# Attention scores on row halves of the array, and a part of the softmax scaling on ScalarE, in a two-layer decoder kernel

## The chip, the cores and the metric

The kernel runs on one core of a Trainium2 chip, in one launch. The metric is the device time of one execution in microseconds (us). A profiled execution gives a span, from the first to the last instruction, and a trace of every engine: TensorE (PE, with its weight loads shown apart as PEld), VectorE (DVE), ScalarE (ACT), GpSimd (POOL) and the queue of SyncE (SP), which issues most DMAs.

## What is computed

Two layers work on 528 tokens (16 learned meta tokens ahead of 512), 1024 wide, in float32. Each layer is a mixer and a squared-ReLU MLP, both between RMS norms. The mixer has two parallel halves: attention with 8 query heads and 2 key/value heads of width 64 and a window of 128 keys, and a short gated convolution. The attention, cut to what matters here:

```python
q = partial_rope(q, cos, sin)
k = partial_rope(k, cos, sin)
s = jnp.einsum('bnqhgd,bnkhd->bnhgqk', qb, kw) * (HEAD_DIM ** -0.5)
s = jnp.where(mask[None, :, None, None], s, -jnp.inf)
m = jnp.maximum(jnp.max(s, axis=-1, keepdims=True), sk)
e = jnp.exp(s - m)
p = e / (jnp.sum(e, axis=-1, keepdims=True) + jnp.exp(sk - m))
o = jnp.einsum('bnhgqk,bnkhd->bnqhgd', p, vw)
```

Queries come in blocks of 128 (and the 16 meta tokens); each block sees its own 128 keys and the 128 ahead of them. Query heads 0 to 3 share key head 0 (g = 0), heads 4 to 7 key head 1 (g = 1). sk is a learned sink per head.

## The kernel before

Activations lie with features on partitions and tokens along the row. Every matrix product runs in a rounded format (float32r); to keep float32 accuracy an operand is split into a rounded part "hi" and a remainder "lo", and a product is the sum hi*hi + hi*lo + lo*hi (`mm3`, L192 to L194). Weights come by DMA in halves of 128 x 512 (`prep`, L134; five buffers `wraw`), are split by a copy on ACT (L107) and a subtraction on DVE (L108), and wait in a pool of prepared tiles; `refill` issues the next ones as tiles are used up. The list `blocks` gives their order: in a layer first the tile of the keys, that of the values, four query tiles, then those of the convolution.

**Queries and keys.** The evacuation of a query tile (`q_evac`, L615) or key tile (`k_evac`, L589) goes through `rope_evac` (L543): ACT copies the product out, four small DMAs on SP swap the rotated rows, DVE multiplies and adds (L559 to L561), and a last step splits the result into hi and lo. A product of scores has only 64 features to sum over. Before the change, both parts were therefore stacked on the 128 partitions: a query head's hi on one half and its lo on the other (`q_parts`, L606), and for the keys the hi of one key head on both halves (`k_hi`) and its lo on both (`k_lo`). One score tile is then two products of depth 128 (`mm2`, L198), which sum all four combinations. The stacking costs two copies and two subtractions of 64 partitions for each query tile (L610, L613) and four and four for a key tile (L598, L603).

**Attention blocks.** A block is (i, g): 128 queries, the four query heads of one key head. `scores` (L660) makes 4 x 2 products of 128x256 into two PSUM banks; DVE adds the mask and takes the maximum (L655); `softmax` (L634) makes the exponentials with their sums on ACT (L644) and then scales each of the four tiles by the reciprocal of its sum on DVE (L650). `transp` (L684) transposes the scaled tiles on PE (L690) and splits them (L279, L280). `attend` (L695) multiplies with the values, four products of 128x512, ACT copies one half of the result (L702) and DVE adds both into z (L703). There are eight blocks in each layer; layer 0 has the meta tokens' block beside them (`meta_scores`, `meta_transp`, `meta_attend`).

**Order.** The mixer has a hand-written plan: a list of matrix products (`plan`), and `put(i, ...)` which hangs an attention step behind product i. Scores run ahead of their transposes by AHEAD blocks; the first scores stand at SCORES_AT = 4, the meta steps at +2, +5 and +6 from there. The delayed part of an evacuation or a softmax is kept in `pend` and emitted behind the next product. From the order written the framework makes each engine's queue with a planner of its own (a simulated timeline), so that queues can differ from the text. In the MLP the tiles `k_hi`, `k_lo` and `vv` and three buffers `tx` are used again as operands of a fast product (`fast`, L908).

Of the kernel before, what the change touches and what calls it, by code (L numbers as in the profile page):

```python
# [8 lines left out]
F32 = mybir.dt.float32  # L9
# [4 lines left out]
P = 128  # L14
D = 1024
KT = D // P
NM = 16
# [19 lines left out]
def trunk_kernel(ctx, tc, xT, gains, sinkb, sinkm, rope, masks, maskm, ident_in, w_in, w_out, w_up, w_down, outT):  # L37
# [22 lines left out]


    k_hi = cp.tile([P, 2, LP], F32R, name="k_hi")
    k_lo = cp.tile([P, 2, LP], F32R, name="k_lo")

# [6 lines left out]
    ct, st, r2, sws = z[:, 4, :], z[:, 5, :], z[:, 7, :], (z[:, 6, :], z[:, 3, :], z[:, 2, :])  # L71
    qm = cp.tile([P, 2, 64], F32R, name="qm")
    mk = cp.tile([P, 256], F32, name="mk")
    mkm = cp.tile([64, NM], F32, name="mkm")
# [6 lines left out]
    for l in range(2):  # L81
        blocks += [("in", l, 512), ("in", l, 640)]
        blocks += [("in", l, P * j) for j in range(4)]
        for jp in range(2):
            for base in (1280, 1792, 768):
                blocks += [("in", l, base + 256 * jp + 128 * m) for m in range(2)]
        blocks += [("out", l, m) for m in range(8)]
        for c in range(NCH):
            if c:
                blocks += [("upx", l, (8 * c + 2 * m, n)) for m in range(4) for n in range(7)]  # L90
            else:
                blocks += [("up", l, 8 * c + m) for m in range(8)]
            blocks += [("down", l, (c, m)) for m in range(8)]
# [40 lines left out]
    def prep(beside=None):  # L134
# [388 lines left out]
    class Mixer:  # L523
# [19 lines left out]
        def rope_evac(self, parts, r, meta=None):  # L543
            t0, t1 = r

            def ev(ps):
# [10 lines left out]
                def rest():  # L557
                    u = tmp(n)
                    DVE.tensor_tensor(u, sw, st[:, t0:t1], ALU.mult)  # L559
                    DVE.tensor_tensor(raw, raw, ct[:, t0:t1], ALU.mult)  # L560
                    DVE.tensor_tensor(raw, raw, u, ALU.add)  # L561
                    parts(raw)
                    if meta is not None:
                        c = 2 * (meta % 2) * NM
                        self.q_parts([qm[:, meta // 2, c + n * NM:c + n * NM + NM] for n in range(2)], raw[:, 0:NM])
                pend.append(rest)
# [22 lines left out]
        def k_evac(self, n):  # L589
            t0, t1 = (RA, RB)[n]  # L590
            cols = slice(PAD + t0, PAD + t1)

            def parts(raw):
                for half in (0, 1):
                    for g in range(2):
                        src = slice(64 * g, 64 * g + 64)
                        dst = src if half == 0 else slice(64 - 64 * g, P - 64 * g)
                        ACT.activation(k_hi[dst, g, cols], raw[src], AF.Copy)  # L598
                for half in (0, 1):
                    for g in range(2):  # L600
                        src = slice(64 * g, 64 * g + 64)
                        dst = src if half == 0 else slice(64 - 64 * g, P - 64 * g)
                        DVE.tensor_tensor(k_lo[dst, g, cols], raw[src], k_hi[src, g, cols].bitcast(F32), ALU.subtract)  # L603
            return self.rope_evac(parts, (t0, t1))

        def q_parts(self, q, raw):  # L606

            for g in range(2):
                src = slice(64 * g, 64 * g + 64)
                ACT.activation(q[g][src], raw[src], AF.Copy)  # L610
            for g in range(2):
                src, dst = slice(64 * g, 64 * g + 64), slice(64 - 64 * g, P - 64 * g)
                DVE.tensor_tensor(q[g][dst], raw[src], q[g][src].bitcast(F32), ALU.subtract)  # L613

        def q_evac(self, j, n):  # L615
            t0, t1 = self.xr[n]
            q = [f[:, j, t0:t1] for f in (f_hi, f_lo)]
            return self.rope_evac(lambda raw: self.q_parts(q, raw), (t0, t1), j if t0 == 0 else None)

# [5 lines left out]
    def mixer(l, mx, mlp_first):  # L625
# [8 lines left out]
        def softmax(S, nh, sink, rows, keys, mxt):  # L634
# [24 lines left out]

        def scores(i, g):  # L660
            S = wp.tile([P, 4, L // 2], F32, tag="x", name="S", bufs=3)[:, :, :256]
# [4 lines left out]
            if i == 0:  # L666
                POOL.memset(S[:, :, :PAD], 0.0)
            for jp in range(2):
                bk = bank()
                for jj in range(2):  # L670
                    j = 2 * jp + jj
                    sc = bk[:, jj * 256:(jj + 1) * 256]
                    q = (f_hi, f_lo)[j % 2][:, 2 * g + j // 2, q0:q0 + 128]
                    mm2(sc, (q, q), (k_hi[:, g, ks], k_lo[:, g, ks]), True, True)
                for jj in range(2):
                    j = 2 * jp + jj
                    masked(S[:, j, keys], bk[:, jj * 256:(jj + 1) * 256][:, keys], mk[:, keys], mxt[:, j:j + 1])
            softmax(S, 4, sb[:, l, 4 * g:4 * g + 4], P, keys, mxt)
            sbufs[(i, g)] = S

        def pT():
            return wp.tile([P, 2, 512], F32R, tag="w", name="p", bufs=2 * CAP)

        def transp(i, g):  # L684
            S = sbufs.pop((i, g))
            pbufs[(i, g)] = []
            for kb in range(2):
# [4 lines left out]
                split(p[:, 0, :], p[:, 1, :], bk)  # L692
                pbufs[(i, g)].append((p[:, 0, :], p[:, 1, :]))

        def attend(i, g):  # L695
            ybk = bank()
            for kb, (phi, plo) in enumerate(pbufs.pop((i, g))):
                mm2(ybk, (vv[:, i + kb, g, :],) * 2, (phi, plo), kb == 0, kb == 1)
            q0 = NM + 128 * i
            rows = slice(g * 64, (g + 1) * 64)  # L700
            y = pT()[:64, 0].bitcast(F32)
            ACT.activation(y, ybk[64:P], AF.Copy)  # L702
            DVE.tensor_tensor(yat[rows, 0:4, q0:q0 + 128], ybk[:64].rearrange("p (j q) -> p j q", j=4),  # L703
                              y.rearrange("p (j q) -> p j q", j=4), ALU.add)

        def meta_scores():
            S = stile(256)[:64].rearrange("p (a b) -> p a b", a=2)
            mxt = tp.tile([P, 4], F32, tag="mx", name="mx", bufs=4)[:64, :2]
            keys = slice(PAD, P)
            POOL.memset(S[:, :, :PAD], 0.0)  # L710
            for g in range(2):
                bk = bank()
                mm2(bk[:64, 0:P], (qm[:, g, :],) * 2, (k_hi[:, g, 0:P], k_lo[:, g, 0:P]), True, True)
                masked(S[:, g, keys], bk[:64, keys], mkm, mxt[:, g:g + 1])
            softmax(S, 2, sm[:, l, :], 64, keys, mxt)
# [112 lines left out]

        order = [(i, g) for i in range(4) for g in range(2)]
        S = [lambda i=i, g=g: scores(i, g) for i, g in order]  # L830
        T = [lambda i=i, g=g: transp(i, g) for i, g in order]
        A = [lambda i=i, g=g: attend(i, g) for i, g in order]
        put(0, mx.v_later[0])
# [74 lines left out]
    def fast(l):  # L908
# [4 lines left out]
        view = lambda t: t.rearrange("p a b -> p (a b)")[:, :4 * n].rearrange("p (k t) -> p k t", k=4)  # L913
        tv = [view(k_hi), view(k_lo), view(vv.rearrange("p a b c -> p a (b c)"))] + [t[:, :, :n] for t in txs[l]]
        T = {"T1": (a_hi[:, 0:4, N1], a_lo[:, 0:4, N1]), "T2": tv[0:2], "T3": tv[2:4], "T4": tv[4:6]}
# [103 lines left out]
    def clear_pad():  # L1019
        for t in (k_hi, k_lo):  # L1020
            POOL.memset(t[:, :, :PAD].bitcast(F32), 0.0)

# [82 lines left out]
```

## Time and profile before

| | us |
|---|---|
| median of 3 runs (1110.06 to 1112.1) | 1111.5 |
| the profiled execution | 1113.09 |
| its span | 1111.3 |
| PE busy | 1079.6 |
| DVE busy | 819.8 |
| ACT busy | 627.0 |

The profile counts an engine as busy while an instruction runs. Products are pipelined: each lasts longer in the records than the distance to the next, so the pace is read from the starts. [...] A wait is the idle time of an engine ahead of an instruction, with what ended it. Idle time of an engine on which nobody waits costs nothing.

### The profile page before, as it was taken

The page shows a single profiled execution, that of the slowest core. Times are in us where ns is not written, and L with a number is a line of the kernel's source. Part 1 is how long each engine was busy: PE and PEld are TensorE (multiplying, and loading weights), DVE is VectorE, ACT ScalarE, POOL GpSimd, SP SyncE. Part 2 cuts the span into 40 slices and gives each one's busy share as a digit, 9 for nine tenths or more (in the row PEclk, how much of TensorE's full clock was granted, in tenths as well). Part 3 has the DMA queues.
Part 4 walks back from the last instruction along what each step waited for, and adds up shares of the span by engine and source line. Part 5 has one row for each costly group of instructions (what it writes and reads, how often), then busy time and mean ns, then how long its engine had stood idle before and what let it go on. Part 6 is the DMA issues. An engine that isn't in the chain of part 4 may idle for free.

```text
span 1111.3 us, 21393 instructions
## 1 busy us (share of the span) xinstructions
PE 1079.6 (97%) x8066; PEld 1038.4 (93%) x8066; DVE 819.8 (74%) x1943; ACT 627.0 (56%) x1510; POOL 11.2 (1%) x46
## 2 busy tenths in 40 slices
PE   8979999999999999999999899999999999999995
PEld 8979999999999999999988899999889989989995
DVE  7997985978486586486598989869947757757835
ACT  8665656675473274176355656666735725724732
POOL 2000000000000000000000000000000000000000
PEclk9999999999999999999998999999999999999998
DMA  9141231342243143234131322222522522522402
GB/s 260 50 126 56 58 96 58 96 134 77 58 131 99 58 122 117 58 105 138 35 112 42 108 59 77 77 76 77 152 67 77 161 67 73 152 73 75 143 1 76
DMA packets 197608, 102.04 MB, mean 92 GB/s; under 512 B 7360, under 2 KB 197456, under 8 KB 197504
## 3 DMA queue, kind: packets, MB, share of 16 engines
q1 hardware_dynamic: 196640, 99.88, 31.1%
q8 instruction: 63, 1.03, 0.4%
q10 hardware_dynamic: 688, 0.58, 0.2%
q14 instruction: 41, 0.34, 0.1%
q0 software_dynamic: 176, 0.21, 0.1%
HBM read 97.88 MB, written 2.10 MB: 90 GB/s over the span
## 4 chain that ended last, share of the span: by engine, by line
PE 83%; DVE 10%; ACT 2%; DMA 2%; issue 2%; SPq 1%; DVEq 0%; ACTq 0%
PE ps L193 26%; PE ps L194 26%; PE ps L192 26%; PE ps L198 2%; PE ps L690 1%; DVE wlo L108 1%; DVE a_lo L334 1%; DVE h L323 1%; DVE acc L276 1%; DMA h<-in_xT 1%; PE ps L231 1%; DMA wraw<-in_w_in 1%; DMA z<-t 0%; ACT whi L107 0%; DVE t L322 0%
## 5 line engine op out<-in xcount | busy, mean ns | idle before, releaser
L193 PE MATMUL ps<-f_lo,whi 128*128 128x256 f32 (+2 forms) x1072 | 326.4, 306 | 0.0
L194 PE MATMUL ps<-f_hi,wlo 128*128 128x256 f32 (+2 forms) x1072 | 326.0, 305 | 0.0
L192 PE MATMUL ps<-f_hi,whi 128*128 128x256 f32 (+2 forms) x1072 | 323.3, 306 | 0.0
L193 PE MATMUL ps<-a_lo,whi 128*128 128x256 f32 (+3 forms) x808 | 232.9, 292 | 1.8 <-DVE a_lo L334 1.7
L192 PE MATMUL ps<-a_hi,whi 128*128 128x256 f32 (+3 forms) x808 | 229.0, 297 | 5.8 <-DVE vv L280 2.6
L194 PE MATMUL ps<-a_hi,wlo 128*128 128x256 f32 (+3 forms) x808 | 231.7, 291 | 0.0
L194 PEld LDWEIGHTS ps<-f_hi,wlo 128*128 128x128 f32 x1072 | 202.0, 189 | 9.2
L108 DVE TENSOR_TENSOR wlo<-wraw,whi 128x512 fp32r<-128x512 f32 x264 | 173.4, 686 | 49.9 <-ACT whi L107 29.0
L193 PEld LDWEIGHTS ps<-f_lo,whi 128*128 128x128 f32 x1072 | 201.4, 188 | 9.4
L192 PEld LDWEIGHTS ps<-f_hi,whi 128*128 128x128 f32 x1072 | 199.9, 188 | 9.3
L107 ACT ACTIVATE whi<-wraw 128x512 fp32r<-128x512 f32 x264 | 153.6, 624 | 86.4 <-PE ps L193 54.6
L193 PEld LDWEIGHTS ps<-a_lo,whi 128*128 128x128 f32 x808 | 155.6, 193 | 5.5 <-DVE a_lo L334 2.6
L192 PEld LDWEIGHTS ps<-a_hi,whi 128*128 128x128 f32 x808 | 151.1, 193 | 9.3 <-DVE vv L280 2.8
L194 PEld LDWEIGHTS ps<-a_hi,wlo 128*128 128x128 f32 x808 | 155.6, 193 | 1.6 <-DVE wlo L108 0.2
L506 DVE TENSOR_TENSOR z<-z,ps 128x272 f32<-128x272 f32 (+2 forms) x78 | 38.0, 487 | 99.1 <-PE ps L194 98.8
L193 PE MATMUL ps<-a_lo,wf 128*128 128x264 f32 (+1 forms) x384 | 108.2, 283 | 0.0
L192 PE MATMUL ps<-a_hi,wf 128*128 128x264 f32 (+1 forms) x384 | 107.9, 283 | 0.0
L107 ACT ACTIVATE wf<-wraw 128x512 fp32r<-128x512 f32 x96 | 59.7, 626 | 84.7 <-PE ps L193 51.8
L194 PE MATMUL ps<-a_hi,wf 128*128 128x264 f32 (+1 forms) x384 | 107.1, 283 | 0.0
L107 ACT ACTIVATE wf<-u 128x512 fp32r<-128x512 f32 x72 | 45.1, 627 | 88.1 <-PE ps L193 73.6
L108 DVE TENSOR_TENSOR wf<-wraw,wf 128x512 fp32r<-128x512 f32 x96 | 65.6, 687 | 11.3 <-ACT wf L107 10.1
L193 PEld LDWEIGHTS ps<-a_lo,wf 128*128 128x128 f32 x384 | 72.2, 188 | 0.1
(175 smaller groups left out, 1815.6 us busy)
## 6 DMA issues: line engine op xcount, KB each, us to landing
wraw<-in_w_up SPq DMA_DIRECT2D x128, 256.0 KB
wraw<-in_w_down SPq DMA_DIRECT2D x128, 256.0 KB
wraw<-in_w_in SPq DMA_DIRECT2D x72, 256.0 KB
wraw<-in_w_out SPq DMA_DIRECT2D x32, 128.0 KB
wraw<-in_w_out SPq DMA_DIRECT2D x16, 256.0 KB
h<-in_xT SPq DMA_DIRECT2D x4, 272.0 KB
h<-in_xT SPq DMA_DIRECT2D x4, 256.0 KB
outT<-h SPq DMA_DIRECT2D x8, 128.0 KB
```

Of the source, the lines that this page charges most:

```text
L107: ACT.activation(hi, raw, AF.Copy)
L108: DVE.tensor_tensor(lo, raw, hi.bitcast(F32), ALU.subtract)
L192: PE.matmul(ps, whi, ahi, start=first, stop=False, skip_group_check=onto)
L193: PE.matmul(ps, whi, alo, start=False, stop=False, skip_group_check=onto)
L194: PE.matmul(ps, wlo, ahi, start=False, stop=last, skip_group_check=onto)
L198: PE.matmul(ps, a[n], b[n], start=first and n == 0, stop=last and n == 1)
L231: PE.matmul(ps, ones[:, which, :], acc, start=True, stop=more is None)
L276: return (eng or DVE).tensor_tensor(acc, acc, sq, ALU.add)
L323: DVE.tensor_tensor(hk, hk, t, ALU.add)
L334: DVE.scalar_tensor_tensor(a_lo[:, k, t0:t1], hk, g, a_hi[:, k, t0:t1].bitcast(F32), ALU.mult, ALU.subtract)
L506: DVE.tensor_tensor(zz, zz, ps, ALU.add)
L690: PE.transpose(bk[:, j * P:(j + 1) * P], S[:, j, kb * P:(kb + 1) * P], ident)
```

## The change

Query tiles now hold head j of both key heads: 64 columns of one and 64 of the other (a new kind "q" of weight block, read by two DMAs a half, each with rows of 64 columns). The hi and lo parts of queries and keys lie in tiles of their own on all 128 partitions, key head 0 on partitions 0 to 63 and key head 1 on 64 to 127, so that a split is one copy and one subtraction. A block is (i, jp): two query heads of each key head. Its scores are three products (hi*hi, hi*lo, lo*hi) of depth 64 for each head, and the products of the two key heads alternate, one on rows 0 to 63 with its bank, the other on rows 64 to 127 with another bank. Of the four scalings two go to ACT. `attend` makes eight products of 256 columns in place of four of 512, and adds to z in two instructions. The meta transposition and attend move by three slots. A constant tile `tx` takes the place of the second key tile among the operands of the fast product.

```diff
-    k_hi = cp.tile([P, 2, LP], F32R, name="k_hi")
-    k_lo = cp.tile([P, 2, LP], F32R, name="k_lo")
+    kk = cp.tile([P, 2, LP], F32R, name="kk")
+    k_hi, k_lo = kk[:, 0, :], kk[:, 1, :]
...
-        blocks += [("in", l, P * j) for j in range(4)]
+        blocks += [("q", l, j) for j in range(4)]
...
+            elif kind == "q":
+                for g in range(2):
+                    last_load[:] = [dma(raw[:, :, 64 * g:64 * g + 64], w_in[l].rearrange("(k p) m -> p k m", p=P)[
+                        :, ks, 256 * g + 64 * sub:256 * g + 64 * sub + 64])]
...
             def parts(raw):
...
+                split(k_hi[:, cols], k_lo[:, cols], raw)
...
-            return self.rope_evac(lambda raw: self.q_parts(q, raw), (t0, t1), j if t0 == 0 else None)
+            return self.rope_evac(lambda raw: split(f_hi[:, j, t0:t1], f_lo[:, j, t0:t1], raw), (t0, t1), j if t0 == 0 else None)
...
                 for i in range(nh):
-                    DVE.tensor_scalar(S[:, i, keys], S[:, i, keys], dn[:, i:i + 1], None, ALU.mult)
+                    if i % 2 and nh == 4:
+                        ACT.activation(S[:, i, keys], S[:, i, keys], AF.Copy, scale=dn[:, i:i + 1])
+                    else:
+                        DVE.tensor_scalar(S[:, i, keys], S[:, i, keys], dn[:, i:i + 1], None, ALU.mult)
...
+        def mm3_heads(outs, q, k):
+
+            for n, (a, b) in enumerate(((0, 0), (0, 1), (1, 0))):
+                for g in range(2):
+                    rows = slice(64 * g, 64 * g + 64)
+                    PE.matmul(outs[g], q[a][rows], k[b][rows], start=n == 0, stop=n == 2)
...
+            bks = [bank() for _ in range(2)]
+            for jj in range(2):
+                mm3_heads([bk[:, jj * 256:(jj + 1) * 256] for bk in bks],
+                          [f[:, 2 * jp + jj, q0:q0 + 128] for f in (f_hi, f_lo)], (k_hi[:, ks], k_lo[:, ks]))
...
+            ps = pbufs.pop((i, jp))
+            for g in range(2):
+                cols = slice(256 * g, 256 * g + 256)
+                for kb, (phi, plo) in enumerate(ps):
+                    mm2(ybk[:, cols], (vv[:, i + kb, g, :],) * 2, (phi[:, cols], plo[:, cols]), kb == 0, kb == 1)
...
-            put(at + 5, meta_transp)
-            put(at + 6, meta_attend)
+            put(at + 8, meta_transp)
+            put(at + 9, meta_attend)
```

## Rows read from the trace of the kernel before

**Rows 1.** The page, part 1: busy us, share and instructions of each engine.
```profile
PE 1079.6 (97%) x8066; PEld 1038.4 (93%) x8066; DVE 819.8 (74%) x1943; ACT 627.0 (56%) x1510; POOL 11.2 (1%) x46
```
**Rows 2.** Waits of PE: for whom, us in total, times, longest.
```profile
PE ps L722 <- DVE s L650: 4.0, 1, 4.0
PE ps L198 <- DVE f_hi L613: 3.9, 1, 3.9
PE ps L192 <- DVE vv L280: 2.6, 1, 2.6
PE ps L690 <- DVE S L650: 2.4, 1, 2.4
...
PE ps L192 <- ACT acc L297: 1.4, 1, 1.4
```
**Rows 3.** Busy time by stretch: us, PE, PEld, DVE, ACT, POOL, granted clock, DMA, GB/s.
```profile
36.00:72.00 36.00, 34.78 (x289) 34.56 (x288) 34.95 (x114) 22.66 (x60) 0.20 (x2) 1.00 0.44 123
74.60:77.90 3.30, 3.30 (x18) 3.30 (x17) 2.76 (x13) 2.89 (x13) 0.10 (x1) 0.50 0.00 0
82.70:88.40 5.70, 5.70 (x21) 4.83 (x21) 2.77 (x13) 0.00 (x0) 0.10 (x1) 0.51 0.31 92
580.00:584.00 4.00, 2.65 (x21) 2.28 (x20) 3.61 (x11) 2.17 (x6) 0.00 (x0) 1.00 0.27 70
600.90:607.00 6.10, 6.08 (x28) 6.08 (x29) 5.97 (x15) 4.90 (x12) 0.00 (x0) 0.50 0.48 136
610.00:624.00 14.00, 10.13 (x85) 9.93 (x85) 13.40 (x48) 8.54 (x26) 0.03 (x1) 1.00 0.32 88
624.20:627.60 3.40, 3.40 (x18) 3.40 (x17) 3.24 (x10) 2.98 (x6) 0.00 (x0) 0.50 0.27 74
```
**Rows 4.** Groups by line and shape on DVE: busy us, mean ns, idle before.
```profile
L280 DVE TENSOR_TENSOR f_lo<-t,f_hi 128x256 fp32r<-128x256 f32 x66 | 27.0, 420 | 3.1 <-ACT f_hi L279 3.1
...
L650 DVE TENSOR_SCALAR S<-S,dn 128x256 f32<-128x256 f32 x48 | 13.7, 349 | 0.2
...
L613 DVE TENSOR_TENSOR f_lo<-t,f_lo 64x256 fp32r<-64x256 f32 x12 | 5.1, 421 | 0.3
```
**Rows 5.** Groups by line and shape on ACT: busy us, mean ns, idle before.
```profile
L644 ACT ACTIVATE S<-S,ng 128x256 f32<-128x256 f32 x48 | 23.8, 499 | 2.9 <-DVE ng L640 2.9
...
L644 ACT ACTIVATION_READ_ACCUMULATOR S<-S,ng 128x1 f32 x64 | 12.1, 189 | 0.0
...
L702 ACT ACTIVATE p<-ps 64x512 f32<-64x512 f32 x16 | 9.6, 597 | 24.0 <-PE ps L198 23.9
...
L763 ACT ACTIVATE z<-u,gt 128x256 f32<-128x256 f32 x12 | 6.1, 506 | 12.7 <-DVE u L757 12.7
```
**Rows 6.** Timeline of DVE at the split of V in layer 1.
```profile
600.32 0.55 DVE L280 TENSOR_TENSOR vv<-ps,vv 128x384 fp32r<-128x384 f32 x1
```
**Rows 7.** Timeline of PE: start, us, instruction; scores, transposes, attend in layer 0.
```profile
55.84 0.28 PE L198 MATMUL ps<-k_hi,f_hi 128*128 128x256 f32 x1
...
56.76 0.28 PE L192 MATMUL ps<-a_hi,whi 128*128 128x256 f32 x1
...
99.68 1.03 PE L690 MATMUL ps<-ident,S 128*128 128x128 f32 x8
100.47 0.36 PE L192 MATMUL ps<-a_hi,whi 128*128 128x256 f32 x1
100.67 0.28 PE L193 MATMUL ps<-a_lo,whi 128*128 128x256 f32 x1
...
106.11 0.62 PE L198 MATMUL ps<-p,vv 128*128 128x512 f32 x2
106.57 0.29 PE L192 MATMUL ps<-a_hi,whi 128*128 128x272 f32 x1
```
**Rows 8.** The page's DMA queues, and busy time of 8 to 24 us.
```profile
q1 hardware_dynamic: 196640, 99.88, 31.1%
...
8.00:24.00 16.00, 14.90 (x102) 14.39 (x102) 14.75 (x33) 14.98 (x38) 0.00 (x0) 0.89 1.09 308
```

More of the change, by code (lines that the diff above doesn't have):

```diff
@@ L563, in rest @@
                     if meta is not None:
-                        c = 2 * (meta % 2) * NM
-                        self.q_parts([qm[:, meta // 2, c + n * NM:c + n * NM + NM] for n in range(2)], raw[:, 0:NM])
+                        cs = slice(meta * NM, meta * NM + NM)
+                        split(qm[:, 0, cs], qm[:, 1, cs], raw[:, 0:NM])
                 pend.append(rest)
@@ L667, in scores, with transp @@
                 POOL.memset(S[:, :, :PAD], 0.0)
-            for jp in range(2):
-                bk = bank()
-                for jj in range(2):
[L671 to L679, printed above, removed]
+            bks = [bank() for _ in range(2)]
[3 more added lines that the diff above has]
+            for g in range(2):
+                for jj in range(2):
+                    n = 2 * g + jj
+                    masked(S[:, n, keys], bks[g][:, jj * 256:(jj + 1) * 256][:, keys], mk[:, keys], mxt[:, n:n + 1])
+            softmax(S, 4, sb[:, l, 4 * jp:4 * jp + 4], P, keys, mxt)
+            sbufs[(i, jp)] = S
         def pT():
             return wp.tile([P, 2, 512], F32R, tag="w", name="p", bufs=2 * CAP)
-        def transp(i, g):
-            S = sbufs.pop((i, g))
-            pbufs[(i, g)] = []
+        def transp(i, jp):
+            S = sbufs.pop((i, jp))
+            pbufs[(i, jp)] = []
             for kb in range(2):
@@ L692, in transp, with attend @@
                 split(p[:, 0, :], p[:, 1, :], bk)
-                pbufs[(i, g)].append((p[:, 0, :], p[:, 1, :]))
-        def attend(i, g):
+                pbufs[(i, jp)].append((p[:, 0, :], p[:, 1, :]))
+        def attend(i, jp):
             ybk = bank()
-            for kb, (phi, plo) in enumerate(pbufs.pop((i, g))):
-                mm2(ybk, (vv[:, i + kb, g, :],) * 2, (phi, plo), kb == 0, kb == 1)
+            ps = pbufs.pop((i, jp))
+            for g in range(2):
+                cols = slice(256 * g, 256 * g + 256)
+                for kb, (phi, plo) in enumerate(ps):
+                    mm2(ybk[:, cols], (vv[:, i + kb, g, :],) * 2, (phi[:, cols], plo[:, cols]), kb == 0, kb == 1)
             q0 = NM + 128 * i
-            rows = slice(g * 64, (g + 1) * 64)
             y = pT()[:64, 0].bitcast(F32)
             ACT.activation(y, ybk[64:P], AF.Copy)
-            DVE.tensor_tensor(yat[rows, 0:4, q0:q0 + 128], ybk[:64].rearrange("p (j q) -> p j q", j=4),
-                              y.rearrange("p (j q) -> p j q", j=4), ALU.add)
+            for g in range(2):
+                cols = slice(256 * g, 256 * g + 256)
+                DVE.tensor_tensor(yat[64 * g:64 * g + 64, 2 * jp:2 * jp + 2, q0:q0 + 128],
+                                  ybk[:64, cols].rearrange("p (j q) -> p j q", j=2),
+                                  y[:, cols].rearrange("p (j q) -> p j q", j=2), ALU.add)
         def meta_scores():
@@ L710, in meta_scores @@
             POOL.memset(S[:, :, :PAD], 0.0)
+            bks = [bank() for _ in range(2)]
+            mm3_heads([bk[:64, 0:P] for bk in bks], (qm[:, 0, :], qm[:, 1, :]), (k_hi[:, 0:P], k_lo[:, 0:P]))
             for g in range(2):
-                bk = bank()
-                mm2(bk[:64, 0:P], (qm[:, g, :],) * 2, (k_hi[:, g, 0:P], k_lo[:, g, 0:P]), True, True)
-                masked(S[:, g, keys], bk[:64, keys], mkm, mxt[:, g:g + 1])
+                masked(S[:, g, keys], bks[g][:64, keys], mkm, mxt[:, g:g + 1])
             softmax(S, 2, sm[:, l, :], 64, keys, mxt)
@@ L827, in put @@
             between.setdefault(i, []).extend(fs)
[L829 to L832, printed above, removed]
+        order = [(i, jp) for i in range(4) for jp in range(2)]
+        S = [lambda i=i, jp=jp: scores(i, jp) for i, jp in order]
+        T = [lambda i=i, jp=jp: transp(i, jp) for i, jp in order]
+        A = [lambda i=i, jp=jp: attend(i, jp) for i, jp in order]
         put(0, mx.v_later[0])
@@ L913, in fast @@
         view = lambda t: t.rearrange("p a b -> p (a b)")[:, :4 * n].rearrange("p (k t) -> p k t", k=4)
-        tv = [view(k_hi), view(k_lo), view(vv.rearrange("p a b c -> p a (b c)"))] + [t[:, :, :n] for t in txs[l]]
+        tv = [view(kk), view(vv.rearrange("p a b c -> p a (b c)"))] + [t[:, :, :n] for t in [tx, *txs[l]]]
         T = {"T1": (a_hi[:, 0:4, N1], a_lo[:, 0:4, N1]), "T2": tv[0:2], "T3": tv[2:4], "T4": tv[4:6]}
```

27 lines of the change are left out of this document (5 added, 22 removed).

## The prediction

> **What bounds the kernel now.** I read the page's engine shares first: TensorE is busy 97% of the span [rows 1]. Where PE is dense, time is the number of products times their pace, and where it is not, time is what PE waits for. So the second view is PE's own list of waits. Four waits lead it, 4.0, 3.9, 2.6 and 2.4 us, each on a VectorE (DVE) instruction of the attention part: the meta scaling (L650), the second half of a query split (L613), the split of V (L280) and the scaling of the first scores (L650) [rows 2]. The third view gives busy time and granted clock by stretch. Two of the waits lie in the mixer of layer 0, two in that of layer 1. In 36 to 72 us DVE is busy 34.95 of 36 us, and in 610 to 624 us 13.40 of 14: DVE is what PE waits for there. [...] Behind a shorter wait, the 1.4 us on L297 in 580 to 584 us, the clock stayed at 1.00 [rows 2, 3]. At half clock half of the time is lost: (3.3 + 5.7 + 6.1 + 3.4)/2 = 9.2 us. With the waits themselves the four places cost some 22 us, 2% of the run.
>
> The sum is made against the profiled execution, 1113.09 us (a span of 1111.3 and 1.8 around it). The median of the runs is 1111.5, so 1.6 is taken off at the end.
>
> **Splits of queries and keys.** A query evacuation issued two copies on ScalarE (ACT) and two subtractions on DVE, each on 64 partitions; now it is one of each on 128. The rows of both kinds last the same, 421 ns for 64x256 and 420 ns for 128x256 [rows 4], so half of it goes: 0.43 us on each engine, eight times a layer. A key evacuation went through four and four instructions of the same form and keeps one and one: 3 x 0.43 = 1.3 us less on each engine, twice a layer. In layer 0 that is 8 x 0.43 + 2 x 1.3 = 6.0 us of DVE work gone ahead of the first transposes (the small meta splits, which halve too, not counted), in a stretch where DVE had 1 us free.
>
> **Softmax scaling.** Two of the four scalings of a block go to ACT: two times 349 ns less on DVE [rows 4]; on ACT the nearest row, a copy with a per-partition scale, takes 506 ns [rows 5]. I cost the 1 us per block on ACT at nothing, because PE's products cover it; if that cover is gone, the fourth rival prices it.
>
> **The four waits.** First transposes of layer 0 (2.4 us): 6.0 us of relief is more than the wait. All of it goes, and its half clock with it: -2.4 - 1.65. Meta transposition (4.0 us): it is moved three slots of the plan later, and the attend that then comes up next needs only the first splits, which are relieved too: -4.0 - 2.85. Split of V in layer 1 (2.6 us): the split ran at 600.32 us behind three key subtractions and a query one that go (1.7 us) [rows 6]; but its transposes end only where the wait begins, 2.6 us ahead of 600.9, and a copy on ACT and the split's own 0.55 us on DVE stay behind them, so about 1.1 us of wait is left and 1.5 goes. The wait left is shorter than the one after which the clock stayed [rows 3], so its half clock goes too: -1.5 - 3.05. Query split in layer 1 (3.9 us): from 610 us on a key evacuation (1.3), three query evacuations (1.3) and one ACT copy ahead of it (0.4) are taken away, -3.0, and 0.9 us stays; by the same comparison its half clock goes: -1.7. Together -10.9 of waits and -9.2 of clock: **-20.1 us**.
>
> **Score products.** A block had 8 products of 128x256, which take 56.76 - 55.84 = 0.92 us, 0.115 each [rows 7]. It now has 12 of depth 64, in six pairs whose partners sit on rows 0 to 63 and 64 to 127 and write different banks. No row of this trace shows two products at once. Low end: each pair costs one product, 6 x 0.115 = 0.69, or -0.23 x 16 blocks = -3.7 us. High end: one after another, 12 x 0.115 = 1.38, or +7.4 us. In between stands the weight load: every product brings its own load of 128 columns, and the only row in which such a load meets a shorter product is the transposes', 8 in 100.47 - 99.68 = 0.79 us, 0.099 each. If loads follow one another at that pace, a block takes 12 x 0.099 = 1.19, and the term is +0.27 x 16 = **+4.3 us**. I take it, since these transposes are the nearest row; the range keeps both ends.
>
> **Turns.** Each block is entered from and left to products of full depth. The nearest row for a turn is the first product behind the transposes, which holds PE for 100.67 - 100.47 = 0.20 us in place of 0.12 [rows 7]: 0.08 more. Two turns in 17 blocks (with meta) make **+2.8 us**; the low end is 0, and the high end is that a product's recorded 0.28 us must run out each time, 0.16 more than its pace, 5.6 us. [...]
>
> **Attend.** Four products of 512 columns at 0.23 (two in 106.57 - 106.11 = 0.46 us [rows 7]) become eight of 256 at 0.115: 0. The sum into z becomes two instructions of 0.42 in place of one of 0.68, 2.6 us more of DVE in all, beside PE's products; with the cover gone it would cost that much.
>
> **Loads of the query weights.** Each half is read by two DMAs in rows of 256 B where one read rows of 512 B: 1024 packets for 512, and 8 more issues a layer on SP. In layer 1 these loads lie far ahead of their use. In layer 0 they fall into 8 to 24 us, where the DMA share is 1.09 [rows 8]: nothing hides there. Low end: time goes by bytes, 0. High end: by packets. 196640 packets took 31.1% of 16 engines' 1111.3 us, 28 ns each [rows 8], so a half costs 512 x 28/16 = 0.9 us more. PE needs three tiles, six halves, in its first groups: 5.4 us. SP's extra issues lie within that. The mean packet cannot tell the two apart; as PE has a buffer of prepared tiles ahead of it (it was busy 14.90 of 16 us in spite of that share), I take a fifth of the high end, **+1.0 us**. [...]
>
> **Sum:** -20.1 + 4.3 + 2.8 + 0 + 1.0 = -12.0, so 1113.1 - 12.0 = 1101.1 for that execution and **1099.5 us** for the median.
>
> **Rivals.** (1) Pairs run together, loads included: the score term is -3.7 in place of +4.3, giving 1091.5. For it: the row halves and the banks differ. Against it: nothing in the trace has two products at once. [...] (2) The row halves do not work at once at all, so the change does not do what it says: +7.4 in place of +4.3, giving 1102.6, and 1105.4 with the dear turns. For it: every matmul row of this kernel starts behind the one before. (3) The waits come back elsewhere. All queues' orders are laid out anew by a planner, and the present waits are places where its guess missed. If half of the 20.1 is kept, 1109.5. For it: even without 6.0 us of work DVE is busy 29 of 36 us in 36 to 72 us. (4) The other side: the transposes wait for ACT. ACT already waits 23.9 us for PE at the copy behind attend (L702) [rows 5], and what stands behind that waits too. If the planner puts a later block's four exponentials ahead of the scalings, ACT needs 0.6 for the copy, 4 x 0.6 (0.5 and a read of 0.19 that overlaps in part) and 2 x 0.5, 4.0 us, while PE has 24 products, 2.8 us: 1.2 us of wait in 14 blocks, 16.8 us, which turns the sum into +4.8 and 1116.3. It decides from 12.0/14 = 0.86 us a block. Against it: PE never waited for ACT in this part before [rows 2].
>
> **Chances.** Forecast 0.38, (1) 0.25, (2) 0.14, (3) 0.13, (4) 0.10. A change within 0.2% (2.2 us) is about what cannot be told from none. Forecast, (1), (2) and a part of (3) are faster by more: 0.82; the rest of (3) is same, 0.07; (4) and a bad (3) are slower, 0.11. The range reaches from (1) with free turns (1113.1 - 23.8 + 2.8 - 1.6, about 1090, a little lower if the turns cost nothing) to (3) and to (2) with dear loads (about 1110): 1089 to 1111. It leaves out (4) and the far edges.
>
> **What would show it.** Right: the four waits gone from PE's list or under 1.2 us, clock 1.00 from 60 to 165 us and from 600 to 700 us, a score block in about 1.2 us. A block in 0.7 us is rival (1), in 1.4 rival (2). Waits of PE on DMA or on a weight cast ahead of 24 us show that the loads were undercosted; waits on an ACT instruction of the scaling line are rival (4). The forecast is wrong if the waits stay with DVE relieved, or if the clock falls though PE does not wait.

## The result and the profile after

The changed kernel takes 1096.99 us (median of 4 runs, 1096.27 to 1097.51), the kernel before 1111.8 beside it: a ratio of 0.9863, 95% interval 0.984 to 0.9887. The profiled execution took 1097.51 with a span of 1095.7, 15.6 us less than before on both counts. The prediction was 1099.5, faster; the time lies in its range.

The page, engine shares and the DMA queue that carries the weights, to set against [rows 1, 8]:

```profile
PE 1074.3 (98%) x8196; PEld 1030.8 (94%) x8196; DVE 801.3 (73%) x1895; ACT 624.6 (57%) x1510; POOL 10.8 (1%) x44
...
q1 hardware_dynamic: 205088, 99.89, 31.9%
```

PE's idle time (span less busy time) falls from 1111.3 - 1079.6 = 31.7 to 21.4 us, so 10.3 of the 15.6 us are waits. The other 5.3 is PE's busy time: it has fallen although PE executes 130 products more, because the half clock is gone (0.50 and 0.51 in the stretches of [rows 3], 1.00 in the rows below). PE's waits, to set against [rows 2]:

```profile
PE ps L196 <- ACT a_hi L380: 1.9, 2, 1.1
PE ps L197 <- DVE a_lo L338: 1.7, 2, 0.9
PE ps L196 <- DVE vv L284: 1.5, 1, 1.5
PE ps L196 <- ACT acc L301: 1.3, 1, 1.3
PE ps L202 <- ACT p L283: 1.2, 1, 1.2
```

Of the four waits only the V split (now L284) is left, 1.5 us in place of 2.6. Waits on the meta scaling, on the query split and on the scaling ahead of the first transposes of layer 0 are gone. New is 1.2 us of attend (L202) on ACT's split of the probabilities, at 631.75 us in layer 1. Busy time by stretch, to set against [rows 3]:

```profile
36.00:72.00 36.00, 36.00 (x309) 34.97 (x309) 31.26 (x112) 21.67 (x72) 0.20 (x2) 1.00 0.46 129
72.00:96.00 24.00, 24.00 (x203) 22.45 (x202) 20.44 (x70) 17.34 (x50) 0.20 (x2) 1.00 0.21 60
590.00:600.00 10.00, 9.35 (x78) 9.35 (x79) 9.19 (x24) 5.40 (x15) 0.10 (x1) 1.00 0.32 90
600.00:640.00 40.00, 38.52 (x335) 36.51 (x334) 34.20 (x130) 27.07 (x85) 0.27 (x2) 1.00 0.36 102
```

The granted clock (the column behind POOL, as a share of full speed) is 1.00 in all of them, and PE is dense from 36 to 96 us. Now PE's timeline at the first scores, to set against [rows 7] (start, us, instruction, times):

```profile
55.58 0.28 PE L197 MATMUL ps<-a_lo,whi 128*128 128x272 f32 x1
55.70 0.28 PE L198 MATMUL ps<-a_hi,wlo 128*128 128x272 f32 x1
55.91 0.50 PE L653 MATMUL ps<-kk,f_hi 64*128 64x256 f32 x4
56.25 0.28 PE L653 MATMUL ps<-kk,f_lo 64*128 64x256 f32 x2
56.37 0.39 PE L653 MATMUL ps<-kk,f_hi 64*128 64x256 f32 x4
...
56.81 0.39 PE L196 MATMUL ps<-a_hi,whi 128*128 128x256 f32 x1
57.03 0.28 PE L197 MATMUL ps<-a_lo,whi 128*128 128x256 f32 x1
```

Twelve products of depth 64 take 56.81 - 55.91 = 0.90 us, and a pair inside takes 56.37 - 56.25 = 0.12, one product's pace: six pairs are 0.69, the other 0.21 lies at the two ends. The product ahead of the block holds PE for 0.21 us in place of 0.12 (55.70 to 55.91), the one behind it for 0.22 (56.81 to 57.03). So one uninterrupted run of row-half products costs 0.09 + 0.21 + 0.10 = 0.40 us beside its products, 0.20 a turn. There are 21 such runs, since the planner puts other products into some blocks: 8.4 us. (The same reading of all 21 in the trace gives 8.7.) The 99 pairs (16 blocks of six, meta three) take 99 x 0.116 = 11.5 us, where 16 blocks of 0.92 and meta's 0.4 took 15.1. So pairs give 3.6 and turns cost 8.4: +4.8 us on PE.

This makes the whole: -10.3 of waits, -9.2 of half clock, +4.8 for scores and turns; -0.9 is left unassigned, and the sum is -15.6.

### The profile page after: what moved, and what is told of

The parts are those of the page before. It is cut to its first block, busy times and chain, and to the rows that moved or that the text cites. A ratio compares the mean times of both kernels' runs of the same rounds, so it can differ in the third digit from the quotient of the medians.

```text
span 1095.7 us, 21642 instructions
## 1 busy us (share of the span) xinstructions
PE 1074.3 (98%) x8196; PEld 1030.8 (94%) x8196; DVE 801.3 (73%) x1895; ACT 624.6 (57%) x1510; POOL 10.8 (1%) x44
## 4 chain that ended last, share of the span: by engine, by line
PE 88%; DVE 7%; ACT 1%; DMA 1%; issue 1%; SPq 1%; DVEq 0%; ACTq 0%
PE ps L196 28%; PE ps L198 28%; PE ps L197 28%; PE ps L202 1%; PE ps L684 1%; PE ps L653 1%; DVE wlo L108 1%; DVE a_lo L338 1%; DVE h L327 1%; DVE acc L280 1%; PE ps L235 1%; DMA h<-in_xT 0%; DVE t L326 0%; DMA z<-t 0%; SPq L558 0%
## 5 line engine op out<-in xcount | busy, mean ns | idle before, releaser
L197 PE MATMUL ps<-a_lo,whi 128*128 128x256 f32 (+3 forms) x808 | 230.2, 289 | 2.0 <-DVE a_lo L338 1.7
L198 PE MATMUL ps<-a_hi,wlo 128*128 128x256 f32 (+3 forms) x808 | 229.2, 288 | 0.1
L196 PEld LDWEIGHTS ps<-a_hi,whi 128*128 128x128 f32 x808 | 148.1, 189 | 9.9 <-ACT a_hi L380 2.3
L197 PEld LDWEIGHTS ps<-a_lo,whi 128*128 128x128 f32 x808 | 152.6, 189 | 5.0 <-DVE a_lo L338 2.6
L198 PEld LDWEIGHTS ps<-a_hi,wlo 128*128 128x128 f32 x808 | 152.9, 189 | 1.4 <-DVE wlo L108 0.3
L108 DVE TENSOR_TENSOR wf<-wraw,wf 128x512 fp32r<-128x512 f32 x96 | 65.7, 688 | 11.5 <-ACT wf L107 10.5
```

The source lines that it names most:

```text
L108: DVE.tensor_tensor(lo, raw, hi.bitcast(F32), ALU.subtract)
L196: PE.matmul(ps, whi, ahi, start=first, stop=False, skip_group_check=onto)
L197: PE.matmul(ps, whi, alo, start=False, stop=False, skip_group_check=onto)
L198: PE.matmul(ps, wlo, ahi, start=False, stop=last, skip_group_check=onto)
```

## The experiments

All times are medians. Differences to the changed kernel are between medians (those of the kernel before were 1110.3 to 1111.8 in all comparisons); its ratio is known to 0.0024, so under some 2.6 us nothing is told apart by time alone. "Runs" are uninterrupted runs of score products in PE's planned order; the meta transposition, which has 64 rows too, is not counted among them. PE busy and idle are those of the one profiled execution. Its clock stands at 0.50 for some 3.4 us between 9 and 15 us in the kernel before and in the changed one. By the page's first slice (27 us, where these two have 0.94) it is below 0.90 in full_depth and before_scale_act and at 0.90 or above in the others, so PE busy differs by 1 us and more between executions for that alone, as an estimate from these shares.

| kernel | us | ratio to before (95%) | runs | PE busy | PE idle |
|---|---|---|---|---|---|
| before | 1111.8 | 1 | | 1079.6 | 31.7 |
| changed | 1097.0 | 0.9863 (0.984 to 0.9887) | 21 | 1074.3 | 21.4 |
| heads_in_turn | 1096.0 | 0.9869 (0.9855 to 0.9882) | 19 | 1074.2 | 20.7 |
| half_by_half | 1101.9 | 0.9913 (0.9899 to 0.9927) | 20 | 1081.0 | 19.9 |
| full_depth | 1100.0 | 0.9906 (0.9892 to 0.992) | 21 | 1078.9 | 20.0 |
| one_between | 1102.1 | 0.9922 (0.9909 to 0.9936) | 32 | 1081.0 | 19.2 |
| blocks_in_twos | 1107.2 | 0.9966 (0.9952 to 0.998) | 16 | 1079.3 | 26.8 |
| rows512 | 1098.9 | 0.9899 (0.9885 to 0.9914) | 21 | 1073.9 | 23.2 |
| scale_dve | 1099.3 | 0.9893 (0.9879 to 0.9906) | 23 | 1075.4 | 21.2 |
| meta_back | 1096.3 | 0.9865 (0.9852 to 0.9879) | 21 | 1073.5 | 21.5 |
| splits_back | 1104.0 | 0.9932 (0.9919 to 0.9946) | 25 | 1080.2 | 23.1 |
| three_back | 1110.7 | 0.9998 (0.9989 to 1.0006) | 26 | 1079.3 | 27.2 |
| before_meta_late | 1105.5 | 0.995 (0.9938 to 0.9962) | | 1073.8 | 28.2 |
| before_scale_act | 1107.9 | 0.9978 (0.9969 to 0.9986) | | 1078.1 | 29.9 |

### Do the halves overlap only when they alternate?

```diff
-            for n, (a, b) in enumerate(((0, 0), (0, 1), (1, 0))):
-                for g in range(2):
+            for g in range(2):
+                for n, (a, b) in enumerate(((0, 0), (0, 1), (1, 0))):
```

> The changed kernel with the twelve score products of a block issued key head by key head (three on rows 0 to 63, then three on rows 64 to 127) in place of alternately. Theory (two products overlap only when the next one issued sits on the other row half): only the one place in six where the halves change can still overlap, so a block takes some 1.3 us of product time in place of 0.69, +0.5 to +0.7 us in 16 blocks: +8 to +11 us, about 1106, and the trace shows starts 0.1 us or more apart within a head. Rival (the order of issue does not matter, or a product of depth 64 simply takes half the time wherever it stands): 0, 1097.

1096.0 us, no more than the changed kernel takes: the theory fell. PE's timeline of the first block of this kernel:

```profile
55.49 0.51 PE L653 MATMUL ps<-kk,f_hi 64*128 64x256 f32 x4
55.82 0.29 PE L653 MATMUL ps<-kk,f_lo 64*128 64x256 f32 x2
...
56.39 0.39 PE L196 MATMUL ps<-a_hi,whi 128*128 128x256 f32 x1
```

A block still takes 56.39 - 55.49 = 0.90 us. The list now reads hi, hi, lo for one half and then hi, hi, lo for the other, and the planner leaves this order in PE's queue; but four f_hi products start first and the two f_lo products together behind them. So the second half's first product, fourth in the list, started with the first.

Next, all six of one half first (the same three products, with the loop over the two query heads inside the loop over the halves):

```diff
-            for jj in range(2):
-                mm3_heads([bk[:, jj * 256:(jj + 1) * 256] for bk in bks],
-                          [f[:, 2 * jp + jj, q0:q0 + 128] for f in (f_hi, f_lo)], (k_hi[:, ks], k_lo[:, ks]))
+            for g in range(2):
+                rows = slice(64 * g, 64 * g + 64)
+                for jj in range(2):
+                    for n, (a, b) in enumerate(((0, 0), (0, 1), (1, 0))):
+                        PE.matmul(bks[g][:, jj * 256:(jj + 1) * 256], (f_hi, f_lo)[a][rows, 2 * jp + jj, q0:q0 + 128],
+                                  (k_hi, k_lo)[b][rows, ks], start=n == 0, stop=n == 2)
```

> The changed kernel with all six score products of a block on rows 0 to 63 issued first, then the six on rows 64 to 127. In the run with three and three the two halves still started together, so the first theory (neighbours must alternate) fell. Theory now (the two row halves take their products from the one list independently, and TensorE looks some products ahead): with six ahead the overlap stays whole or nearly so: 0 to +2 us, 1096 to 1099, and both halves' first products start together. Rival (it looks only three or four ahead): the second half starts two or three products late, +0.25 to +0.35 a block, +4 to +6 us, and the starts show it.

1101.9 us, 4.9 more: the rival came true. The starts of the first block:

```profile
56.29 0.50 PE L669 MATMUL ps<-kk,f_hi 64*128 64x256 f32 x2
56.63 0.28 PE L669 MATMUL ps<-kk,f_lo 64*128 64x256 f32 x1
56.63 0.50 PE L669 MATMUL ps<-kk,f_hi 64*128 64x256 f32 x4
56.97 0.28 PE L669 MATMUL ps<-kk,f_lo 64*128 64x256 f32 x2
57.09 0.40 PE L669 MATMUL ps<-kk,f_hi 64*128 64x256 f32 x2
57.33 0.28 PE L669 MATMUL ps<-kk,f_lo 64*128 64x256 f32 x1
57.53 0.39 PE L196 MATMUL ps<-a_hi,whi 128*128 128x256 f32 x1
```

Two products of the first half run alone; at 56.63 the second half's first product, seventh in the list, starts together with the third: it started four places ahead and not five. The block takes 57.53 - 56.29 = 1.24 us, 0.34 more. Sixteen such blocks would make 5.4; the planner breaks some up so that the halves meet sooner, and all runs of the trace together take 4.5 us more than those of the changed kernel. (A stretch at a lower clock in layer 1, a mean of 0.72 over 6 us, adds to PE's busy time; see the last section.) The last three products of the second half run alone, 0.12 us apart (57.09 to 57.33 for two): a product of depth 64 by itself is no shorter than one of full depth, so what the changed kernel saves is the overlap.

### What do full depth and turns cost?

```diff
-                    PE.matmul(outs[g], q[a][rows], k[b][rows], start=n == 0, stop=n == 2)
+                    PE.matmul(outs[g], q[a], k[b], start=n == 0, stop=n == 2)
```

> The changed kernel with every score product taken over all 128 rows: twelve products of full depth a block, no row halves and so no turns. This changes the scores (each becomes the sum over both key heads). Theory (pairs run at one product's pace, 0.115, and each uninterrupted run of row-half products costs 0.40 us for its turns): products 12 x 0.115 = 1.38 in place of 0.69, +11 us, and 21 runs x 0.40 = 8.4 us given back: +2.6, about 1099.6; the product ahead of and behind each block keeps its usual pace. Rival (my forecast's sizes: loads at 0.099, turns 0.08 each way, 2.8 us in all): +0.19 x 16 - 2.8 = 0, 1097. The time alone barely separates them, the starts in the trace do.

1100.0 us, 3.0 more. PE's timeline at the first block:

```profile
56.08 0.29 PE L198 MATMUL ps<-a_hi,wlo 128*128 128x272 f32 x1
56.20 0.63 PE L653 MATMUL ps<-kk,f_hi 128*128 128x256 f32 x4
...
57.62 0.28 PE L196 MATMUL ps<-a_hi,whi 128*128 128x256 f32 x1
57.74 0.28 PE L197 MATMUL ps<-a_lo,whi 128*128 128x256 f32 x1
```

The block takes 57.62 - 56.20 = 1.42 us, 0.118 a product, and its neighbours keep 0.12. So the slow starts at the ends belong to the depth-64 products. In sum 16 x 1.42 = 22.7 against 16 x 0.69 + 21 x 0.40 = 19.4: +3.3 us, where 3.0 was measured. The pace of 0.099 that the forecast took for the loads does not show: a product takes 0.118 as it does elsewhere.

Then one product of full depth more, between the first six and the last six of each block:

```diff
+                if jj == 0:
+                    PE.matmul(bks[0][:, 256:512], f_hi[:, 2 * jp, q0:q0 + 128], k_hi[:, ks], start=True, stop=True)
```

> The changed kernel with one more product of full depth (128 x 256, its result written over at once) between the first six and the last six score products of each block: 32 uninterrupted runs of row-half products in place of 21, and 16 products more. Theory (0.40 us a run): 11 x 0.40 + 16 x 0.115 = +6.2 us, about 1103.2. Rival A (the forecast's 0.16 us a run): 11 x 0.16 + 1.8 = +3.6, 1100.6. Rival B (turns are free and the slow starts seen belong to something else): +1.8, 1098.8.

1102.1 us, 5.1 more, between the theory and rival A in time. PE's busy time is 6.7 higher, and its waits came out 2.2 lower (attend's wait on ACT fell from 1.2 to 0.2). The timeline of one block:

```profile
55.17 0.50 PE L653 MATMUL ps<-kk,f_hi 64*128 64x256 f32 x4
55.51 0.28 PE L653 MATMUL ps<-kk,f_lo 64*128 64x256 f32 x2
55.72 0.39 PE L669 MATMUL ps<-kk,f_hi 128*128 128x256 f32 x1
56.03 0.50 PE L653 MATMUL ps<-kk,f_hi 64*128 64x256 f32 x4
```

Three pairs take 55.72 - 55.17 = 0.55 us where 3 x 0.115 = 0.35 would do, and the product between them 0.31 where 0.12 would do. So the break costs 0.20 + 0.19 = 0.39 us: 0.40 a run, by a kernel made to show it.

### Fewer turns

Two blocks are handed out at a time, the first of them one slot later than in the changed kernel; the fourth buffer of scores takes the place of `tx0` (the lines of the buffers are left out).

```diff
-        for n in range(AHEAD):
-            put(at + n, S[n])
+        put(at + 1, S[0], S[1])
+        put(at + 3, S[2], S[3])
...
-            if n + AHEAD < 8:
-                put(pos + 1, S[n + AHEAD])
+            if n % 2 == 1 and n + 3 < 8:
+                put(pos + 1, S[n + 3], S[n + 4] if n + 4 < 8 else (lambda: None))
```

> The changed kernel with two score blocks handed out at a time (a fourth score buffer takes the place of a constant tile), which leaves 16 uninterrupted runs of row-half products in place of 21. Theory: 5 x 0.40 = 2.0 us less, about 1095, if DVE and ACT swallow two softmaxes in a row. Rival (the bunched work behind the scores makes PE wait for DVE or ACT): 0 to +5 us, with a new wait of PE in the stretch of the scores.

1107.2 us, 10.2 more. The longest of PE's waits in this kernel:

```profile
PE ps L201 <- ACT p L282: 5.7, 4, 2.3
```

The rival came true, at twice its price: four waits of attend on ACT's split of the probabilities, 5.7 us in place of 1.2, and the clock at 0.83 to 0.93 in the 10-us stretches from 90, 100, 590 and 650 us on. Five runs fewer (2.0 us) don't pay for that.

### The loads of the query weights

```diff
-                for g in range(2):
-                    last_load[:] = [dma(raw[:, :, 64 * g:64 * g + 64], w_in[l].rearrange("(k p) m -> p k m", p=P)[
-                        :, ks, 256 * g + 64 * sub:256 * g + 64 * sub + 64])]
+                last_load[:] = [dma(raw, w_in[l].rearrange("(k p) m -> p k m", p=P)[:, ks, P * sub:P * sub + P])]
```

> The changed kernel with each tile of query weights read by one DMA in rows of 512 B, as before. The columns then belong to other heads, so that the queries are other numbers; every instruction behind the load is the same. Theory (the first products that use these loads start within 0.02 us of their old times, so the 256-B rows cost PE nothing): 0, 1097. Rival (the forecast's share of the dearer packets): -1 us; at its high end -5 us.

1098.9 us, not faster: nothing is to be had. This kernel's weight queue, by the page:

```profile
q1 hardware_dynamic: 196640, 99.88, 31.5%
```

By bytes the same, the shares give 0.319 x 16 x 1095.7 = 5592 us of engine time with the short rows and 0.315 x 16 x 1097.1 = 5529 without. As an estimate from them, with the mean packet's 28 ns for a row of 512 B, 8192 rows (230 us) became twice as many at (230 + 63)/16384 = 18 ns. (The shares are rounded, which leaves about 1 ns open.) PE doesn't notice: the first product of 256 columns starts at 23.16 us in the kernel before, at 23.15 in the changed kernel and at 23.65 in this one, so long rows bring it no sooner.

### Which part took the waits away?

One part undone at a time, first the scaling:

```diff
-                    if i % 2 and nh == 4:
-                        ACT.activation(S[:, i, keys], S[:, i, keys], AF.Copy, scale=dn[:, i:i + 1])
-                    else:
-                        DVE.tensor_scalar(S[:, i, keys], S[:, i, keys], dn[:, i:i + 1], None, ALU.mult)
+                    DVE.tensor_scalar(S[:, i, keys], S[:, i, keys], dn[:, i:i + 1], None, ALU.mult)
```

> The changed kernel with all four scalings of a softmax on DVE again (one part undone). DVE gets 2 x 0.35 us a block back, 11 us over 16 blocks, ACT gives up 2 x 0.5. Theory (it is the splits and the later meta slot that took the waits away, and DVE has 4.7 of 36 us free in 36 to 72 us): 0 to +2, and the 1.2 us wait on ACT's split of the probabilities in layer 1 goes. Rival (this part is what relieves DVE ahead of the first transposes): the wait on the scaling of the first scores comes back, with its stretch at half clock, in both layers: +4 to +8 us.

1099.3 us: 2.3 more, at the edge of what can be told. No wait on the scaling came back, and the one on ACT's split of the probabilities did not go (1.5 us at one place), so ACT's scalings are not its cause. Two runs of score products more account for 0.8.

```diff
-            put(at + 8, meta_transp)
-            put(at + 9, meta_attend)
+            put(at + 5, meta_transp)
+            put(at + 6, meta_attend)
```

> The changed kernel with the meta transposition and attend in their old slots, three earlier (one part undone). Theory (the later slot is what took the 4.0 us wait away, since DVE is still busy 19.6 of 20 us in 60 to 80 us): a wait of PE on the meta scaling of 2 to 4 us comes back, with 1 to 3 us of half clock: +3 to +7 us. Rival (6 us less DVE work would have done it by itself): 0, 1097.

1096.3 us: the rival came true. In the old slot the meta transposition waits 1.0 us in place of 4.0, the clock stays at 1.00, and the time is the same.

```diff
+    def split64(hi, lo, src):
+        for g in range(2):
+            r = slice(64 * g, 64 * g + 64)
+            ACT.activation(hi[r], src[r], AF.Copy)
+        for g in range(2):
+            r = slice(64 * g, 64 * g + 64)
+            DVE.tensor_tensor(lo[r], src[r], hi[r].bitcast(F32), ALU.subtract)
...
-                split(k_hi[:, cols], k_lo[:, cols], raw)
+                for _ in range(2):
+                    split64(k_hi[:, cols], k_lo[:, cols], raw)
...
-            return self.rope_evac(lambda raw: split(f_hi[:, j, t0:t1], f_lo[:, j, t0:t1], raw), (t0, t1), j if t0 == 0 else None)
+            return self.rope_evac(lambda raw: split64(f_hi[:, j, t0:t1], f_lo[:, j, t0:t1], raw), (t0, t1), j if t0 == 0 else None)
```

> The changed kernel with the splits of queries and keys issued as before in number: two copies and two subtractions of 64 partitions for a query, four and four for a key (each written twice), so 6 us of DVE work come back ahead of the first transposes of each layer. Theory (this part took away three of the four waits): waits on the first transposes in layer 0 and on the query and V splits in layer 1 come back, with half clock: +6 to +13 us. Rival (the scaling moved to ACT and the later meta slot leave room enough): 0 to +2 us.

1104.0 us, 7.0 more; four runs of score products more make 1.6 of it. PE's longest waits, and busy time by stretch, of this kernel:

```profile
PE ps L196 <- DVE vv L284: 2.9, 1, 2.9
PE ps L693 <- POOL u L756: 2.3, 1, 2.3
```
```profile
594.00:600.00 6.00, 6.00 (x38) 6.00 (x39) 5.91 (x15) 4.07 (x10) 0.00 (x0) 0.72 0.39 114
630.00:640.00 10.00, 7.71 (x52) 7.40 (x53) 6.61 (x28) 7.73 (x24) 0.24 (x1) 0.83 0.10 27
```

The V split is back at 2.9 us, and transposes (L693) of layer 1 wait 2.3 (the row puts it on GpSimd; what they read is the scaled scores), both with the clock below 1.00 behind them. But nothing came back in layer 0, and the query split of layer 1 didn't either: the time lies in the theory's range, by other waits than it named. All three at once (the three diffs above together):

> The changed kernel with three parts undone at once: the scalings on DVE, the meta steps in their old slots, the splits in their old number of instructions. The score products on two row tiles, the attend halves and the query loads stay. Theory (each part covers for the others; what is left of the change costs +4.5 for products and turns): the waits and half clock of before come back: +13 to +20 us against the changed kernel, 1110 to 1117, at or above the time before. Rival (the costs simply add: 2 + 0 + 7): +9, about 1106.

1110.7 us, 13.7 more, the time of before (0.9998); five more runs make 2.0 of it. PE's longest waits, and the stretch behind the first:

```profile
PE ps L727 <- DVE s L644: 5.1, 1, 5.1
PE ps L196 <- DVE vv L284: 2.4, 1, 2.4
PE ps L690 <- DVE S L644: 2.2, 1, 2.2
```
```profile
76.00:84.00 8.00, 4.21 (x23) 3.67 (x23) 4.21 (x17) 2.01 (x11) 0.10 (x1) 0.61 0.22 66
```

Undone singly the parts cost 2.3, -0.7 and 7.0, in sum 8.6; together 13.7. They cover for each other in layer 0: the meta wait comes back whole only when more than one of them is undone. (Its profiled execution was one of its fastest, 1108.3.) But these are not the four waits of before. The 2.2 us on L690 lie in layer 1, at 636 us; the query split does not wait; and the first transposes of layer 0 do not wait, though DVE is busy for 35.29 us of 36 to 72 us again (34.95 before). DVE comes sooner to the scaling that they read; the first row is from the kernel before, the second from this one:

```profile
72.72 0.69 DVE L650 TENSOR_SCALAR S<-S,dn 128x144 f32<-128x144 f32 x3
```
```profile
68.40 0.69 DVE L644 TENSOR_SCALAR S<-S,dn 128x144 f32<-128x144 f32 x3
```

Of these 4.3 us, 1.6 belong to the execution, in which PE is as much ahead by then; 2.7 are left, more than the 2.4 of the wait. In the changed kernel DVE comes to this scaling at 62.95 us, with the splits alone undone at 69.89. So the splits are worth some 7 us of a lead of 10, but the rest of it is enough to clear this wait. Where the rest comes from was not separated.

Last, one part alone, put into the kernel before, first the later slot of the meta steps:

```diff
-            put(at + 5, meta_transp)
-            put(at + 6, meta_attend)
+            put(at + 8, meta_transp)
+            put(at + 9, meta_attend)
```

> The kernel before with only the meta transposition and attend moved three slots later. Theory (the waits are queueing on a full DVE, which three parts relieve, each of them enough in part): the 4.0 us wait on the meta scaling and its 2.85 us of half clock go, the other three stay: -4 to -7 us, 1104 to 1107. Rival (as undoing this part in the changed kernel, which cost nothing): 0, 1111.

1105.5 us, 4.8 less than the 1110.3 beside it. PE's waits, and busy time by stretch:

```profile
PE ps L198 <- DVE f_hi L613: 3.9, 1, 3.9
PE ps L192 <- DVE vv L280: 2.6, 1, 2.6
...
PE ps L690 <- DVE S L650: 2.0, 1, 2.0
```
```profile
72.00:100.00 28.00, 26.50 (x206) 25.51 (x207) 25.88 (x98) 18.73 (x64) 0.20 (x2) 1.00 0.20 58
```

The meta wait is gone and the other three stand, with the clock at 1.00 from 72 to 100 us: a step that is worth nothing beside the others is worth 4.8 us alone. Then the scaling:

```diff
-                    DVE.tensor_scalar(S[:, i, keys], S[:, i, keys], dn[:, i:i + 1], None, ALU.mult)
+                    if i % 2 and nh == 4:
+                        ACT.activation(S[:, i, keys], S[:, i, keys], AF.Copy, scale=dn[:, i:i + 1])
+                    else:
+                        DVE.tensor_scalar(S[:, i, keys], S[:, i, keys], dn[:, i:i + 1], None, ALU.mult)
```

> The kernel before with only two of the four scalings of a block on ACT. DVE has 0.7 us less a block, 2.8 us less by the first transposes of a layer. Theory (relief of any kind shortens the waits): the first transposes' wait (2.4 us and 1.65 of half clock) goes and the meta wait shrinks: -4 to -10 us, 1101 to 1107. Rival (undoing it in the changed kernel cost only 2 us, so alone it gives as little): 0 to -2, 1109 to 1111.

1107.9 us, 2.4 less: near the rival in time, with the theory in kind. The first transposes and the meta step wait 1.7 us each in place of 2.4 and 4.0; the two waits of layer 1 are as before.

## Why the prediction was right, point by point

The time is in range for the reason that the prediction named, the waits and their half clock. That it came so near is in part luck: of the terms below, scores and turns were wrong by -7.9 and +5.6 us, which cancel for the most part.

**Waits and clock, -20.1.** Measured, in the profiled execution: -10.3 of idle time (forecast -10.9) and all 9.2 us of half clock (half of the stretches at 0.50 and 0.51 in [rows 3]; the clock is 1.00 in those places now). The size stands; the reasons stand in part. Of the four places:
- V split: 1.1 us was to stay, 1.5 did, more than the 1.2 that was named as a sign of being right, with the clock at 1.00 (on that, see the last section). With the splits undone it is 2.9 and 2.4; in the variants that keep them merged 1.5 to 2.4, so the planner's order decides as well.
- First transposes of layer 0: gone, as said. That 6.0 us less of splits does it was not shown: with the splits undone the wait stayed away, and with all three parts undone too. In the kernel before, the scaling alone took it from 2.4 to 1.7 and the meta slot alone to 2.0.
- Meta: gone. The later slot was given first; undone, it costs nothing as long as the splits and the scaling relieve DVE. Either reason would have done. With all three undone it is back, 5.1.
- Query split of layer 1: 0.9 was to stay, nothing did. It didn't come back with the splits undone either, alone or with the other two, so the instructions that I counted off are not what takes it away. What the rest of the new layout does there was not separated; this stays open.

**Score products, +4.3.** The wrong value was taken. The pairs run together, loads included: -3.6, the low end (-3.7) and rival 1's mechanism. Two loads, one for each half, fit into 0.12 us here (of a block's loads in PEld two start at 56.14 us and the next at 56.25), so loads of the two halves do not follow one another at the transposes' 0.099.

**Turns, +2.8.** Mis-sized: 8.4, beyond the high end of 5.6. A turn takes 0.20 us, not 0.08 to 0.16, since products on both sides of the border slow down, and there are 21 runs and not 17, since the planner breaks blocks up. The row behind the transposes was no turn of this kind: its tiles are 128*128 on both sides. The slow products stand at both ends of a run and are gone at full depth (0.12); what holds them there was not shown. Scores and turns together were to cost 7.1 and cost 4.8: two errors of opposite sign. Rival 1 had the pairs right, but its time had the turns at 2.8.

**Attend and scaling, 0.** The rows of the changed kernel on DVE and ACT (busy us, mean ns, idle before):

```profile
L701 DVE TENSOR_TENSOR z<-ps,p 64x256 f32<-64x256 f32 x32 | 13.3, 416 | 4.5 <-ACT p L698 4.1
L638 DVE TENSOR_SCALAR S<-S,dn 128x256 f32<-128x256 f32 x24 | 7.4, 349 | 0.2
```
```profile
L636 ACT ACTIVATE S<-S,dn 128x256 f32<-128x256 f32 x24 | 10.8, 502 | 0.0
```

416 and 502 ns where 0.42 us and 506 ns were taken. Rival 4's wait on the scaling line of ACT did not occur; attend waits 1.2 us once for ACT's split, and it does so with the scaling on DVE too.

**Loads, +1.0.** 0: the first groups end no later (23.15 us). The price of a row of 256 B, as estimated from the queue's shares 18 ns against half of 28, is (18 x 2 - 28)/28 = 29% more by the byte.

Put with these sizes, the sum is -10.3 - 9.2 + 4.8 = -14.7 against -15.6 measured. Rivals 2 and 3 fell in the changed kernel; the kernels with the splits undone show what (3) looks like, with a wait of 2.2 or 2.3 us on transposes of layer 1 where there was none.

## What to carry to other kernels

A layout that packs two shallow products side by side is paid for at its borders: here 0.20 us each way against 0.23 us saved in a block. So count the uninterrupted runs in the planned order, not the blocks in the source. The score products by themselves lost 4.8 us; the gain came from waits of PE, and undoing three reliefs of VectorE together takes it back. Waits on a full engine are not owned by one cause: price the parts of a relief together, and test them both ways, undone in the new kernel and alone in the old one. Bunching work to spare turns moved the wait to the engine behind (5.7 us on ACT).

## What the runs showed that was not expected

- TensorE started a product of the other row half out of the list's order: four places ahead, and not five (the starts of the run half by half, the seventh of its first block with the third, at 56.63 us).
- The length of a wait alone did not tell whether the clock falls behind it. Busy time by stretch around the V split, of the kernel at full depth (a wait of 2.0 us) and of the one half by half (1.8 us):

```profile
590.00:594.00 4.00, 2.05 (x17) 1.81 (x16) 3.46 (x10) 3.35 (x10) 0.10 (x1) 1.00 0.14 34
594.00:600.00 6.00, 6.00 (x53) 6.00 (x52) 5.40 (x14) 2.99 (x8) 0.10 (x1) 1.00 0.44 125
```
```profile
590.00:594.00 4.00, 2.19 (x19) 1.95 (x18) 3.21 (x9) 3.32 (x11) 0.10 (x1) 0.99 0.11 25
594.00:600.00 6.00, 6.00 (x40) 6.00 (x40) 5.39 (x13) 2.57 (x6) 0.00 (x0) 0.72 0.46 131
```

Both stand still for about as long and then run without a gap; one keeps a clock of 1.00, the other has a mean of 0.72 over the next 6 us. My step "a wait shorter than the one of 1.4 us keeps the clock" was not put to the test: 1.5 us were left at the V split, and the clock stayed all the same. In the nine kernels that keep the splits merged, one profiled execution each, the wait at the V split is 1.5 to 2.4 us; the clock fell behind it in two (half_by_half, 1.8 us, and blocks_in_twos, 2.4) and stayed at 1.00 in six (the changed kernel, heads_in_turn, full_depth, scale_dve, meta_back and, at 2.3 us, rows512). So that this half clock went is in part luck too.
